# First MLP pair by plain products, and a down projection that begins without residuals

## Chip, cores and metric

One core of a Trainium2 chip. The metric is the device time of one execution in microseconds (us). Five engines run side by side, each with its own instruction stream: TensorE (PE, weight loads PEld), VectorE (DVE), ScalarE (ACT), GpSimd (POOL) and SyncE (SP, which here only issues DMAs).

## What is computed

One inference step of a hybrid backbone with one trunk layer: 1152 tokens (128 of context, 1024 latent), 1024 channels, all float32.

```python
def trunk_layer(x, mod, lp, lam, lam_init, ctx_k, ctx_v, rope):
    shift1, scale1, gate1, shift2, scale2, gate2 = jnp.split(mod, N_MOD, axis=-1)
    h = rmsnorm(x, lp['w_norm1']) * (1.0 + scale1) + shift1
    mix, k, v = token_mixer(h, lp, lam, lam_init, ctx_k, ctx_v, rope)
    x = x + gate1 * mix
    h = rmsnorm(x, lp['w_norm2']) * (1.0 + scale2) + shift2
    up = dwconv(h @ lp['w_up'], lp['w_ffn_dw'])
    ff = (jax.nn.silu(up[..., :D_FF]) * up[..., D_FF:]) @ lp['w_down']
    x = x + gate2 * ff
    return x, k, v
```

The token mixer (attention and a convolution, merged by gates, with an output projection at its end) is not touched. The change lies in the part from `gate1 * mix` on: the second norm, the MLP's up projection to 2 x 2816 channels, a depthwise convolution of width 3 over tokens, the gate, and the down projection.

## The kernel before

**Layout and precision.** Activations lie with channels on the 128 partitions and tokens along the free axis, in three thirds of 384 tokens (`n` = 0, 1, 2; third 0 holds the context tokens, so it has two segments with different modulation). Each float32 operand is split into a rounded part `hi` (ScalarE's cast) and a remainder `lo` (a subtraction on VectorE or POOL), and a product is three matmuls: hi·hi, hi·lo, lo·hi. Weights come in units of 128 x 1024: SP's queue loads `raw`, ScalarE casts `whi` (L180), POOL subtracts `wlo` (L182); `prep_to` does this some units ahead, with four buffers each for `whi` and `wlo`.

**Order.** The program is written in the order wanted, with a clock of *ticks*: `run` and `block` tick after a number of matmuls, and `defer(t, f)` emits the step `f` `t` ticks later. A background list `bg` is emitted at `bg_rate` per tick, and `flush` ticks until nothing is pending. At build time a scheduler with a timing model of its own fixes the order of each engine's instructions; it may move them against the written order (`pin` limits that to 144 instructions on PE and 24 on VectorE). On the chip each engine runs its own instructions in that order and waits at the first whose inputs aren't there.

**Output projection** (`out_and_ffn`, `wo_unit`). Eight units for thirds 0 and 1, then the same eight for third 2 (24 matmuls each, a tick per 8). VectorE adds the gated result to the residual `x1[n]` (`resid`, L1230), ScalarE squares it (L1243), VectorE adds up the squares (L1244). A copy of `x1` goes to DRAM (`xscr`) for the last residual add. During the first eight units VectorE also reduces modulation vectors from their weight matrix (`ada2`, L1192).

**Second norm.** For each third the sum of squares is summed over partitions by TensorE (`stat_cols`, L252: three products with one column each), VectorE adds epsilon, POOL takes the power, VectorE makes a diagonal (L265), TensorE broadcasts it into PSUM (`stat_bcast`, L273). Then VectorE multiplies (`mulr`, L1300) and ScalarE scales and shifts in place (`affine`, L1306). All steps for thirds 0 and 1 are deferred by 1, 2, 3, ... ticks into the output projection of third 2.

**Up projection in pairs** (`mlp`, `pair`). Pair `i` makes 128 channels of each half of `w_up` for all tokens. For thirds 0 and 1 it takes the 2 x 2 scheme of Strassen and Winograd: the two halves of the contraction, the two channel blocks and the two thirds form 2 x 2 blocks, and seven products of 12 matmuls (`block`) take the place of eight. For this `mlp_operands` makes seven operands from quarters of the normalised tokens: B11, B22, B21 as they are, nT1, T2, nT3, nT4 as sums and differences (VectorE and POOL), each then split into hi and lo (`split`, L1322, L1323). The sums of weight quarters are VectorE's too (`fetch_pair`, L164). Third 2 is computed plainly in four blocks `c1` to `c4`. Seven PSUM banks rotate; VectorE combines the products (`tt`, L1472), then come the depthwise filter `dw` (ScalarE L1432, VectorE L1434), silu (L1530) and the product of both halves (L1532), which goes to DRAM (`fscr`). After pair 0, `stage` starts the reduction of the last modulation vector, which gates the MLP's result, in the background (L1192, in bursts of four).

**Down projection** (`down`, then the last group with the final norm). The 22 channel blocks of `fscr` are taken in groups: first 2, then five times 4. Each is loaded (L1565), cast (L1566) and split (L1568) by `ff_prep`; group 0 multiplies 24 banks with 6 matmuls each, the later groups 24 with 12 each; `resid` adds each bank, gated, to `x1`. The residuals `x1` are loaded back from `xscr` during the last pair (`reload`, L1551), into the slots of operands that are used up by then. PSUM gives five banks here.

Of the kernel before, what the change touches and what calls it, by code (L numbers as in the profile page):

```python
# [8 lines left out]
F32 = mybir.dt.float32  # L9
# [7 lines left out]
NCTX = 128  # L17
# [4 lines left out]
KC = 8  # L22
# [61 lines left out]
def _w_order():  # L84
# [8 lines left out]
    ffn = [f"w{i}_{u}" for i in range(NFF) for u in range(4)] + down  # L93
# [16 lines left out]
class Kernel:  # L110
# [1069 lines left out]

    def ada2(self, count, more=True):
        nc = self.nc
        for _ in range(count):
            u, raw = self.ada_raw.pop(0)
            ty, k = divmod(u, KC)
            b = self.vec[:, V_ADA + 16 + u:V_ADA + 17 + u]
            step = self.junk.shape[-1]
            for c in range(2):
                acc = self.mod[:, ty, k, c:c + 1]
                for o in range(0, 1024, step):  # L1190
                    sl = slice(o, o + step)
                    nc.vector.tensor_tensor_reduce(out=self.junk, in0=raw[:, sl], in1=self.cbc[c][:, sl], scale=0.5,  # L1192
                                                   scalar=acc if o else b, op0=ALU.mult, op1=ALU.add, accum_out=acc)
            if more:
                self.defer(3, lambda: self.ada_fetch(1))


    def out_and_ffn(self):
        tc, nc, A = self.tc, self.nc, self.A
        vec = self.vec  # L1200
        with tc.tile_pool(name="p3", bufs=1) as p3:
# [35 lines left out]

            def square(n, j):
                if j == 0:
                    nc.scalar.activation(out=acc[n], in_=x1[n][:, 0], func=AF.Square)  # L1240
                else:
                    sq = self.sm.tile([128, CH], F32, tag="dg", name="sq", bufs=2)
                    nc.scalar.activation(out=sq, in_=x1[n][:, j], func=AF.Square)  # L1243
                    nc.vector.tensor_tensor(out=acc[n], in0=acc[n], in1=sq, op=ALU.add)  # L1244

# [31 lines left out]
            for i, f in enumerate(op["steps"]):  # L1277
                self.defer(1 + i, f)
            for j in range(KC):
                wo_unit(j, (2,))  # L1280
            self.flush()
            for i, f in enumerate(self.third_operands(x1, acc, op)):
                self.defer(1 + i, f)
            self.mlp(p3, x1, op, hx, slot, small, flat, resid)

    def norm_steps(self, acc, bank, col_bank, box):
# [8 lines left out]
        return [a, a2, b]  # L1295

# [12 lines left out]
    def mlp_operands(self, x1, acc, hx):  # L1309
# [16 lines left out]
        s0 = self.norm_steps(acc[0], lambda: self.spare[:, 0], lambda: self.spare[:, 2], box[0])  # L1326
        s1 = self.norm_steps(acc[1], lambda: self.spare[:, 1], lambda: self.spare[:, 2], box[1])
        steps = [s0[0], s1[0], s0[1], s1[1], s0[2], s1[2]]
        x, y = x1[0], x1[1]

        def half(q):
            up, dn = slice(2 * q, 2 * q + 2), slice(4 + 2 * q, 6 + 2 * q)

            def m(rows):
                def f():
                    for n in range(2):
                        self.mulr(x1[n], rows, box[n]["r"])
                    for n in range(2):
                        for k in range(rows.start, rows.stop):
                            self.affine(n, x1[n], k)  # L1340
                return f
# [461 lines left out]
```

## Time and profile before

| | us |
|---|---|
| median of 3 runs | 1833.96 |
| lowest and highest | 1832.01, 1837.11 |
| the profiled execution | 1833.82 |
| its span, first to last instruction | 1832.0 |
| TensorE busy in it | 1689.6 |

The profile is of one execution. A stretch is named by its start and end in us from the first instruction. "Idle before <- releaser" gives how long an engine had nothing to run before an instruction and what ended that; engine, line and tile of the releaser stand behind the arrow. TensorE's clock is the granted one, as a share of full speed; it has two levels, 0.5 and 1.

### The profile page before, as it was taken

The numbers are of one execution on the slowest core, as the hardware profiler recorded it, in microseconds if no ns is written. First come the engines' busy times: TensorE is split into PE (matmuls) and PEld (weight loads), VectorE is DVE, ScalarE is ACT, GpSimd is POOL, SyncE is SP. The second block draws the span as 40 slices with busy tenths as digits, with TensorE's granted clock in tenths as the row PEclk, the third lists the DMA queues.
The fourth block names the chain that finished last, engine by engine and source line by source line (L and its number), as shares of the span: only waits on it lengthen the run. The fifth ranks groups of instructions, "written<-read, shape, count | busy, mean of one in ns | idle before, by whom it ended". The sixth has DMA issues, their size and how long they took to land. (4 is left out here: it accounts for less than half of the span.)

```text
span 1832.0 us, 25186 instructions
## 1 busy us (share of the span) xinstructions
PE 1689.6 (92%) x9874; PEld 1646.4 (90%) x9874; DVE 1265.6 (69%) x1620; ACT 681.6 (37%) x1073; POOL 820.2 (45%) x479
## 2 busy tenths in 40 slices
PE   5989899989989999899985998999999996999997
PEld 3889889988989999789985998999999996999997
DVE  5858985697795762786879878786766856433335
ACT  4423444354553563211254433334333433111111
POOL 2545782674872422543345533444444543233211
PEclk8999999999999999999987999999999998999999
DMA  8264233433425325665831322221212226222202
GB/s 316 75 186 144 90 94 96 146 80 116 119 80 196 116 95 193 196 214 193 293 129 37 100 95 90 71 85 67 84 54 72 79 100 245 97 99 70 89 12 104
DMA packets 101295, 220.50 MB, mean 120 GB/s; under 512 B 9876, under 2 KB 60728, under 8 KB 98744
## 3 DMA queue, kind: packets, MB, share of 16 engines
q1 hardware_dynamic: 48720, 136.66, 21.8%
q10 hardware_dynamic: 51592, 79.08, 13.6%
q0 software_dynamic: 864, 3.15, 0.5%
q8 instruction: 78, 1.28, 0.3%
q14 instruction: 41, 0.34, 0.1%
HBM read 161.55 MB, written 57.30 MB: 119 GB/s over the span
## 5 line engine op out<-in xcount | busy, mean ns | idle before, releaser
L182 POOL TENSOR_TENSOR wlo<-raw,whi 128x1024 fp32r<-128x1024 f32 x124 | 328.0, 2646 | 532.7 <-ACT whi L180 515.3
L230 PE MATMUL f<-h1h,whi 128*128 128x384 f32 x680 | 233.2, 345 | 4.6 <-ACT gt L602 3.2
L230 PE MATMUL f<-h1l,whi 128*128 128x384 f32 x680 | 233.9, 344 | 0.0
L1434 DVE SCALAR_TENSOR_TENSOR X<-X,vec,X 128x1153 f32<-128x1153 f32 x88 | 164.6, 1871 | 98.4 <-ACT X L1432 97.6
L230 PE MATMUL f<-h1h,wlo 128*128 128x384 f32 x680 | 231.5, 341 | 0.0
L180 ACT CAST whi<-raw 128x1024 fp32r<-128x1024 f32 x126 | 131.8, 1046 | 231.8 <-PE f L230 50.0
L639 DVE SCALAR_TENSOR_TENSOR conv<-glu,vec,conv 128x967 f32<-128x967 f32 x120 | 199.2, 1660 | 1.1
L182 POOL TENSOR_TENSOR wlo<-rawx,whi 128x1024 fp32r<-128x1024 f32 x44 | 112.3, 2559 | 88.6 <-ACT whi L180 80.1
L652 POOL TENSOR_TENSOR conv<-conv,tap 128x200 f32<-128x200 f32 x120 | 115.5, 963 | 69.4 <-ACT tap L646 66.9
L230 PEld LDWEIGHTS f<-h1h,whi 128*128 128x128 f32 x680 | 130.0, 192 | 6.6 <-ACT gt L602 3.9
L230 PEld LDWEIGHTS f<-h1l,whi 128*128 128x128 f32 x680 | 130.4, 192 | 0.4
L230 PEld LDWEIGHTS f<-h1h,wlo 128*128 128x128 f32 x680 | 129.8, 191 | 0.2
L781 DVE TENSOR_REDUCE mx<-S 128x1 f32<-128x1152 f32 (+1 forms) x72 | 88.6, 1231 | 31.4 <-PE S L775 31.4
L783 ACT ACTIVATE e<-S,mx 128x1152 f32<-128x1152 f32 (+1 forms) x72 | 81.3, 1129 | 69.8 <-DVE mx L781 58.1
L230 PE MATMUL T<-ff,whi 128*128 128x384 f32 x360 | 94.1, 339 | 14.2 <-ACT ff L1566 11.6
L646 ACT ACTIVATE tap<-glu,vec 128x200 f32<-128x200 f32 x120 | 55.5, 462 | 106.0 <-POOL conv L652 89.2
L180 ACT CAST whi<-rawx 128x1024 fp32r<-128x1024 f32 x44 | 46.0, 1051 | 129.1 <-DVE rawx L164 60.2
L230 PE MATMUL f<-ff,whi 128*128 128x384 f32 x340 | 88.5, 338 | 0.0
L774 PE MATMUL S<-K,q 128*128 128x384 f32 (+1 forms) x200 | 69.1, 346 | 13.9 <-ACT e L783 13.9
L230 PEld LDWEIGHTS T<-ff,whi 128*128 128x128 f32 x360 | 66.1, 191 | 15.4 <-ACT ff L1566 12.0
L1230 DVE SCALAR_TENSOR_TENSOR hx<-T,g,hx 128x128 f32<-128x128 f32 (+1 forms) x79 | 38.9, 513 | 57.8 <-PE T L230 57.6
L1230 DVE SCALAR_TENSOR_TENSOR hx<-f,g,hx 128x384 f32<-128x384 f32 (+1 forms) x76 | 37.6, 514 | 57.6 <-PE f L230 57.6
(419 smaller groups left out, 4890.7 us busy)
## 6 DMA issues: line engine op xcount, KB each, us to landing
raw<-in_wst SPq DMA_DIRECT2D x104, 512.0 KB, 4.0
X<-scr_fscr SPq DMA_DIRECT2D x22, 576.0 KB, 4.7
scr_fscr<-X SPq DMA_DIRECT2D x22, 512.0 KB, 2.9
scr_gscr<-gate ACTq DMA_DIRECT2D x48, 192.0 KB, 2.0
tg<-scr_gscr SPq DMA_DIRECT2D x24, 384.0 KB, 4.3
ada<-in_ada SPq DMA_DIRECT2D x8, 1024.0 KB, 9.9
araw<-in_ada ACTq DMA_DIRECT2D x16, 512.0 KB, 4.1
K<-scr_kscr ACTq DMA_DIRECT2D x4, 1920.0 KB, 7.8
```

The lines of the kernel that those rows point to most:

```text
L180: nc.scalar.copy(hi, raw)
L182: eng.tensor_tensor(out=lo, in0=raw, in1=hi.bitcast(F32), op=ALU.subtract)
L230: nc.tensor.matmul(out, lhsT=a, rhs=b, start=(i == 0), stop=(i == n - 1))
L639: t = nc.vector.scalar_tensor_tensor(out=o, in0=glu[:, j:j + CSPLIT], scalar=w[:, j:j + 1], in1=o, op0=ALU.mult, op1=ALU.add)
L646: nc.scalar.activation(out=p, in_=glu[:, CSPLIT + j:CONVW + j], func=AF.Copy, scale=w[:, j:j + 1])
L652: t = nc.gpsimd.tensor_tensor(out=o, in0=o, in1=p, op=ALU.add)
L774: nc.tensor.matmul(S[:, j, :cw], lhsT=qt[:, c, o:o + 128], rhs=self.K[:, c, ks], start=True, stop=False)
L781: nc.vector.tensor_reduce(out=mx[:, 1:2], in_=src, axis=AX.XY, op=ALU.min)
L783: nc.scalar.activation(out=e[:, :w].rearrange("p (a b) -> p a b", a=nk), in_=src, func=AF.Exp, scale=-1.0, bias=mx[:, 1:2], accum_out=self ...
L1230: nc.vector.scalar_tensor_tensor(out=d, in0=ps[:, o:o + ln], scalar=gate[:, j, c:c + 1], in1=d, op0=ALU.mult, op1=ALU.add)
L1434: nc.vector.scalar_tensor_tensor(out=y[:, :L], in0=u[:, t:t + L], scalar=w[:, t:t + 1], in1=y[:, :L], op0=ALU.mult, op1=ALU.add)
```

## The change

- Pair 0 no longer uses the seven products. `first_pair` multiplies the unchanged weights `fa0` and `fb0` with the tokens as they are: twelve blocks, thirds 0, 1, then 2. Its operands are B11, B21, B12 and B22, made by `h2_rows` during the output projection of third 2; for third 0 ScalarE writes `hi` directly from the scale-and-shift, and VectorE makes the same value again for the remainder.
- The sums of quarters (`op["sums"]`) follow in the ticks of `first_pair`, after and between the steps for third 2; all their splits are now on VectorE. nT4 takes the buffer of B12 at the end.
- The norm's steps start at tick 4 instead of 1; the flush before `mlp` is gone; third 2's squares are summed by TensorE as each is made.
- The background reduction begins after pair 1 and goes piece by piece, one each 10 ticks.
- Loads of `fscr` are issued by `ff_load`: the first two from SP at the end of the pair before the last, the others from POOL, each as soon as its buffer's last user is written down.
- Group 0 of the down projection writes `x1` by ScalarE (`begin`), and POOL issues accumulating DMAs that add the residuals from `xscr`, two rows of a third at a time. `reload` is gone.

```diff
-    ffn = [f"w{i}_{u}" for i in range(NFF) for u in range(4)] + down
+    ffn = up[:2] + [f"w{i}_{u}" for i in range(1, NFF) for u in range(4)] + down
...
             def square(n, j):
-                if j == 0:
+                if n == 2:
+                    sq = self.sm.tile([128, CH], F32, tag="dg", name="sq", bufs=2)
+                    nc.scalar.activation(out=sq, in_=x1[n][:, j], func=AF.Square)
+                    self.defer(2, lambda: add_square(sq, j))
+                elif j == 0:
...
             for i, f in enumerate(op["steps"]):
-                self.defer(1 + i, f)
+                self.defer(4 + i, f)
             for j in range(KC):
                 wo_unit(j, (2,))
-            self.flush()
-            for i, f in enumerate(self.third_operands(x1, acc, op)):
-                self.defer(1 + i, f)
+            for i, f in enumerate(self.third_operands(x1, sums, op)):
+                self.defer(2 + i, f)
+            for i, f in enumerate(op["sums"]):
+                self.defer(6 + i, f)
             self.mlp(p3, x1, op, hx, slot, small, flat, resid)
...
+    def h2_rows(self, n, x, rows, r, hi, lo, direct):
+        nc = self.nc
+        self.mulr(x, rows, r)
+        if direct:
+            for k in range(rows.start, rows.stop):
+                for o, ln, c in self.segs(n):
+                    nc.scalar.activation(out=hi[:, k - rows.start, o:o + ln], in_=x[:, k, o:o + ln], func=AF.Identity,
+                                         scale=self.s2[:, k, c:c + 1], bias=self.h2s[:, k, c:c + 1])
+                    nc.vector.tensor_scalar(out=x[:, k, o:o + ln], in0=x[:, k, o:o + ln],
...
+        else:
+            for k in range(rows.start, rows.stop):
+                self.affine(n, x, k)
+            nc.scalar.copy(hi, x[:, rows])
+        nc.vector.tensor_tensor(out=lo, in0=x[:, rows], in1=hi.bitcast(F32), op=ALU.subtract)
...
+        steps += [plain(n, q, d) for d in range(2) for q in range(2) for n in range(2)]
...
+            def o2():
+                tt(x[:, up], x[:, up], y[:, up], ALU.subtract)
+                split("nT1", up, x[:, up], nc.vector)
+            def o4():
+                tt(x[:, up], x[:, up], y[:, dn], ALU.add)
+                split("T2", up, x[:, up], nc.vector)
+                tt(x[:, dn], x[:, dn], x[:, up], ALU.subtract)
+            def o5():
+                tt(y[:, up], y[:, up], y[:, dn], ALU.subtract)
+                split("nT3", up, y[:, up], nc.vector)
+            def o7():
+                if q == 0:
+                    op["nT4"] = op["B12"]
                 split("nT4", up, x[:, dn], nc.vector)
...
-            self.bg = [lambda: self.ada2(1)] * 8 + [lambda: nc.vector.tensor_copy(self.g2, self.mod[:, 3])]
-            self.bg_rate = (1, 20)
+            self.bg = [f for _ in range(8) for f in self.ada2_steps()]
+            self.bg += [lambda: nc.vector.tensor_copy(self.g2, self.mod[:, 3])]
+            self.bg_rate = (1, 10)
...
+        def first_pair():
...
+            for n in range(NCH):
+                for u in range(2):
+                    for k0 in (0, 4):
+                        quarter(u, n, k0)
+                if n == 1:
+                    self.prep_to(self.pos + 2)
+            up = flat(slot("X2"))
...
+            for u in range(2):
+                for n in range(NCH):
+                    to_u(up[u], n, lambda d, t: nc.scalar.copy(d, bank[u, n][:, t]))
+            self.flush()
+            for f in ops["late"]:
+                f()
+            start()
...
+            dw(0, up[0], ya)
+            nc.scalar.activation(out=ya[:, :1153], in_=ya[:, :1153], func=AF.Silu)
+            dw(NFF, up[1], yb)
...
-            if i == 0:
+            if i == 1:
                 stage()
+            if i == NFF - 2:
+                ff_load(), ff_load()
...
-        def reload(n):
-            x1[n] = hx()
-            nc.sync.dma_start(out=x1[n], in_=A["xscr"][n])
+        def ff_load():
+            c = parts_at["stage"]
+            parts_at["stage"] += 1
+            if c < NFF:
+                raw = late["x2"][:, T * (c % 2):T * (c % 2) + T]
+                (nc.sync if c < 2 else nc.gpsimd).dma_start(out=raw, in_=A["fscr"][c])
...
+        def begin(n, j, ps):
+            if j == 0:
+                x1[n] = hx()
+            for o, ln, c in self.segs(n):
+                nc.scalar.activation(out=x1[n][:, j, o:o + ln], in_=ps[:, o:o + ln], func=AF.Copy,
+                                     scale=self.g2[:, j, c:c + 1])
+            if j % 2:
+                sl = slice(j - 1, j + 1)
+                nc.gpsimd.dma_start(out=x1[n][:, sl], in_=A["xscr"][n][:, sl], accum_op=ALU.add)
...
-                    resid(n, j, ps, self.g2)
+                    if g:
+                        resid(n, j, ps, self.g2)
+                    else:
+                        begin(n, j, ps)
...
-        for i in range(NFF):
+        first_pair()
+        for i in range(1, NFF):
             pair(i)
```

## Rows read from the trace of the kernel before

**Rows 1.** the page's first part: busy us, share of the span, instructions

```profile
PE 1689.6 (92%) x9874; PEld 1646.4 (90%) x9874; DVE 1265.6 (69%) x1620; ACT 681.6 (37%) x1073; POOL 820.2 (45%) x479
```

**Rows 2.** stretches: length, busy us per engine (count), TensorE clock, DMA share, GB/s

```profile
920.00:967.00 47.00, 39.62 (x221) 39.29 (x219) 33.41 (x50) 28.24 (x48) 21.16 (x11) 0.89 0.36 123
967.00:1020.00 53.00, 34.31 (x155) 32.01 (x154) 42.59 (x43) 23.22 (x32) 34.13 (x22) 0.77 0.12 41
1020.00:1046.00 26.00, 22.93 (x121) 22.00 (x120) 25.79 (x29) 11.44 (x13) 10.44 (x4) 0.93 0.42 131
1046.00:1300.00 254.00, 243.62 (x1383) 240.47 (x1382) 200.02 (x245) 93.78 (x106) 109.97 (x42) 0.99 0.24 81
...
1520.00:1545.00 25.00, 10.75 (x44) 9.64 (x43) 14.37 (x17) 9.29 (x9) 9.72 (x4) 0.69 0.90 332
1545.00:1780.00 235.00, 235.00 (x1353) 235.00 (x1353) 92.97 (x178) 42.59 (x43) 70.08 (x30) 1.00 0.23 80
```

**Rows 3.** TensorE's timeline: start us, us, line, operation [idle us before <- releaser]

```profile
929.55 1.44 PE L252 MATMUL S<-cols,acc 128*128 128x1 f32 x6 [7.38 <-DVE acc L1244]
...
936.64 0.72 PE L252 MATMUL S<-cols,acc 128*128 128x1 f32 x6
937.23 0.42 PE L230 MATMUL O<-ml,whi 128*128 128x384 f32 x1
```

**Rows 4.** TensorE's waits in 960:1046, 1046:1300, 1515:1560: us, times, longest

```profile
PE f L1442 <- POOL wlo L182: 5.7, 1, 5.7
...
PE O L1442 <- DVE X L1472: 5.1, 2, 4.7
...
PE T L1442 <- POOL wlo L182: 1.8, 1, 1.8
...
PE T L230 <- ACT ff L1566: 11.6, 1, 11.6
PE T L230 <- DVE hx L1230: 2.4, 1, 2.4
```

**Rows 5.** timeline of SP's queue before the down projection

```profile
1517.21 1.26 SPq L1551 DMA_DIRECT2D hx<-scr_xscr  x2
...
1519.06 0.97 SPq L1565 DMA_DIRECT2D X<-scr_fscr  x2
```

**Rows 6.** timelines of VectorE and POOL: start us, us, operation, count

```profile
944.70 6.99 DVE L1300 TENSOR_TENSOR X<-X,S 128x768 f32<-128x768 f32 x8
...
964.13 5.13 DVE L1323 TENSOR_TENSOR hx<-X,hx 128x768 fp32r<-128x768 f32 x2
...
1111.11 2.72 DVE L1192 CUSTOM_DVE_ANT_0 X<-X,vec 128x512 f32<-128x512 f32 x1
...
948.55 2.41 POOL L182 TENSOR_TENSOR wlo<-raw,whi 128x1024 fp32r<-128x1024 f32 x1 [4.20 <-ACT whi L180]
...
964.08 6.83 POOL L1323 TENSOR_TENSOR op<-X,op 128x768 fp32r<-128x768 f32 x3 [1.11 <-ACT op L1322]
```

**Rows 7.** single lines of the kernel: duration ns min/median/max, starts, forms

```profile
L1323 DVE TENSOR_TENSOR hx<-X,hx x6: 939/1644/2619, 952.7 to 990.6; 128x768 fp32r<-128x768 f32 x6
...
L288 DVE TENSOR_SCALAR mn<-mn,s,h1s x32: 333/468/2631, 26.4 to 76.1; 128x384 f32<-128x384 f32 x16, 128x128 f32<-128x128 f32 x8, 128x256 f32<-128x256 f32 x8
...
L164 DVE TENSOR_TENSOR raw<-raw x22: 674/679/693, 960.1 to 1480.3; 128x512 f32<-128x512 f32 x22
...
L180 ACT CAST whi<-raw x126: 1027/1048/1067, 16.4 to 1763.4; 128x1024 fp32r<-128x1024 f32 x126
...
L182 POOL TENSOR_TENSOR wlo<-raw,whi x124: 2339/2406/4181, 52.2 to 1764.5; 128x1024 fp32r<-128x1024 f32 x124
...
L1434 DVE SCALAR_TENSOR_TENSOR X<-X,vec,X x88: 1407/1423/3543, 1019.3 to 1524.9; 128x1153 f32<-128x1153 f32 x88
...
L1505 ACT COPY X<-f x7: 472/473/484, 1017.4 to 1419.4; 128x384 f32<-128x384 f32 x7
```

**Rows 8.** the view of DMA issues: count, KB each, us to landing

```profile
X<-in_crow POOLq DMA_DIRECT2D x2, 512.0 KB, 6.7
```

More of the change, by code (lines that the diff above doesn't have):

```diff
@@ L1244, in square, with add_square @@
                     nc.vector.tensor_tensor(out=acc[n], in0=acc[n], in1=sq, op=ALU.add)
+            def add_square(sq, j):
+                if j == 0:
+                    sums["ps"] = self.spare[:, 2]
+                for t in range(3):
+                    nc.tensor.matmul(sums["ps"][:, t:t + 1], lhsT=sq[:, t * 128:(t + 1) * 128], rhs=self.col_mean,
+                                     start=j == 0 and t == 0, stop=j == KC - 1 and t == 2)
             cb, ar = flat(hx()), flat(hx())
@@ L1325, in mlp_operands, with part @@
         box = [{}, {}]
[L1326 to L1327 removed]
+        s0, s1 = (self.norm_steps(acc[n], b, b, box[n]) for n, b in
+                  enumerate((lambda: self.spare[:, 0], lambda: self.spare[:, 1])))
         steps = [s0[0], s1[0], s0[1], s1[1], s0[2], s1[2]]
         x, y = x1[0], x1[1]
+        def part(name, q):
+            rows = slice(2 * q, 2 * q + 2)
+            return op[name][:, rows], op[name][:, rows.start + 4:rows.stop + 4]
@@ new lines, in alloc, with plain, f @@
+        def alloc():
+            for name, make in (("B11", hx), ("nT1", hx), ("T2", hx), ("B22", hbt), ("nT3", hbt), ("B21", hbt),
+                               ("B12", hbt)):
+                operand(name, make)
+        def plain(n, q, down):
+            def f():
+                if not op:
+                    alloc()
+                hi, lo = part(f"B{2 if down else 1}{n + 1}", q)
+                rows = slice(4 * down + 2 * q, 4 * down + 2 * q + 2)
+                self.h2_rows(n, x1[n], rows, box[n]["r"], hi, lo, n == 0)
+            return f
@@ L1343, in o1 @@
-            def o1():
-                if q == 0:
-                    for name, make in (("B11", hx), ("nT1", hx), ("T2", hx), ("B22", hbt), ("nT3", hbt),
-                                       ("B21", hbt), ("nT4", hbt)):
-                        operand(name, make)
-                split("B11", up, x[:, up], nc.vector)
-            def o2():
-                nc.vector.tensor_tensor(out=x[:, up], in0=x[:, up], in1=y[:, up], op=ALU.subtract)
-                split("nT1", up, x[:, up], nc.vector)
@@ L1379, in third_operands @@
+        h0, h1 = half(0), half(1)
+        return {"steps": steps, "ops": op, "sums": [f for ab in zip(h0[0], h1[0]) for f in ab], "late": [h0[1], h1[1]]}
+    def third_operands(self, x1, sums, ops):
         nc = self.nc
+        op = ops["ops"]
         hi = op["h"] = self.hb.tile([128, KC, CH], F32R, tag="hb", name="h2h")
@@ L1403, in mlp, with edges @@
         late = {}
+        def edges(tiles):
+            for t in tiles:
+                for c0 in (0, 129, 1154):
+                    nc.gpsimd.memset(t[:, c0:c0 + 1], 0.0)
+            return tiles
         def start():
```

132 lines of the change are left out of this document (64 added, 68 removed).

## The prediction

> **What bounds the kernel now.** The page's first part comes first: TensorE is busy for 92% of the span [rows 1], so the time is TensorE's, and a change can win only its waits and its slow stretches. The view of stretches shows where they lie [rows 2]: from 1545 us to 1780 us TensorE is busy all the time at clock 1.00; between 920 and 1046 us, and again between 1520 and 1545 us, it is not. The steady price is 235.00 us / 1353 = 0.1737 us for a matmul of 384 columns. For each stretch the idle time is its length less TensorE's busy time, and the slowness, which the lower granted clock leaves, is busy time less count x 0.1737 us; TensorE's waits name what ended the longest idle pieces [rows 4]. All by [rows 2]:
>
> - 920 to 967 us (output projection of the third tokens): idle 47 - 39.6 = 7.4, nearly all before the column sums of squares [rows 3]; slow 39.62 - 221 x 0.1737 = 1.2.
> - 967 to 1046 us (first two MLP pairs): idle 79 - 34.31 - 22.93 = 21.8, the longest for a weight split of POOL (5.7 [rows 4]); slow 57.24 - 276 x 0.1737 = 9.3.
> - 1046 to 1300 us: idle 10.4; slow 243.62 - 1383 x 0.1737 = 3.4.
> - 1520 to 1545 us (start of the down projection): idle 14.2, of it 11.6 for ScalarE's cast of the MLP's result and 2.4 for VectorE's eviction [rows 4]; slow 10.75 - 44 x 0.1737 = 3.1.
>
> That is 70.8 us in all, and the change touches each of the four. Stages before 920 us stay as they are.
>
> **Part 1, the statistics.** TensorE's first wait, 7.4 us, is for the last sum of squares of token third 0 [rows 3]. This step moves from the first tick to the fourth. A tick is 8 matmuls here, so 24 x 0.1737 = 4.2 us of work goes ahead of it, and 3.2 us of waiting stay: gain 4.2. The squares of the third tokens are now summed by TensorE as they come: ten sets of three one-column products in place of three. A set holds the matmuls up by 0.59 us (936.64 to 937.23 us [rows 3]), so 7 x 0.59 = 4.1 us are added. The additions that VectorE loses by it gain nothing by themselves.
>
> **Part 2, plain products in the first pair.** Seven products of 12 matmuls and four blocks of 12 for the third tokens, 132, become twelve blocks, 144: 12 x 0.1737 = 2.1 us added for certain. In return the first blocks need only normalised tokens, no sums of quarters. For these VectorE has, while the third tokens' projection runs (192 matmuls, 33 us), per quarter two multiplications by the broadcast and two subtractions at 0.94 and four scale-and-shift pieces at about 0.4 (the same operation took 0.33 to 0.47 in the first norm) [rows 7]: 4 x 5.4 = 21 us, begun when the broadcasts are out, which I put 8 us behind the column sums of 929.55 us [rows 3], near 938. With the projection's evictions beside it, that ends at about 965 us: the operands are there when TensorE comes. ScalarE's part is covered: it idles 19 of the 47 us [rows 2].
>
> Then TensorE has eight blocks, 16.7 us, on token thirds 0 and 1. In them VectorE makes the third tokens' operands (8 operations) and the quarter sums and their splits (14), 22 x 0.94 = 21 us in alternation, begun some 5 us in. The third operands are done after 16 to 20 us: 0 to 3 us late. The weight sums of pair 1 stand behind the quarter sums, at 26 us; sum (0.68), cast (1.05) and POOL's split (2.41) [rows 7] make 30 us, where TensorE wants them at 25: 5 us late. In pair 1 the depthwise filters of pair 0 (four of 1.42 [rows 7]) stand before the later weight sums: 0 to 6, say 2. With 3 us at the lower clock behind these waits, 12 of the 31.1 us stay: gain 19. Bounds: 3 stay if all operands are early (gain 28), 24 if VectorE lags (gain 7).
>
> VectorE and POOL hinder each other: two of its subtractions took 5.13 us at 964.13 us while POOL ran three of its own [rows 6], against 0.94 each at best [rows 7]; its multiplications by a PSUM operand kept 0.87 each through POOL's work at 948.55 us [rows 6]. The change takes 6 splits of 2.4 us off POOL here and gives them to VectorE. The Trainium skill (SBUF — State Buffer, "Who interferes with whom") states that a VectorE instruction with two SBUF inputs and a GpSimd instruction that reads SBUF exclude each other for the whole instruction, and that one with a single SBUF input does not; the trace agrees with both (5.13 and 0.87 us). The rival that follows from it is the first below.
>
> **Part 3, modulation spread out.** After pair 0 the last modulation vector is reduced in the background, four pieces in a burst each 20 ticks; now one piece each 10 ticks, from the end of pair 1. At 1111.11 us such a piece took 2.72 us ahead of a weight sum [rows 6], and TensorE waited 1.8 us for the weight; its longest wait here, 4.7 us for VectorE's eviction, lies among such pieces too [rows 4]. Only these two carry the mark of the bursts: 6.5 us and part of the slow 3.4. New backlog from pair 1 eats some: gain 5, bounds 0 and 10.
>
> **Part 4, start of the down projection.** The load behind TensorE's wait of 11.6 us was issued at 1519.06 us, after two reloads of residuals on SP's queue [rows 5], in a stretch with the DMA engines 90% busy [rows 2]. The change takes the reloads away and issues the first two loads a pair (23 us) earlier, so the casts fit into the last pair. That cover needs POOL, whose split of the odd part (2.4 us or more [rows 7]) must find room among the weight splits of the last pair; a weight split takes 2.41 and four fall in its 23 us. Late next is ScalarE: it now drains the first group's 24 banks, 8 x (2 + 1 + 1) copies at 0.47, 15 us, with eight casts of 1.05, 8.4 [rows 7], and the last pair's silu and filter ahead of them: 24 us or more beside TensorE's 144 x 0.1737 = 25 us. And a cast that waits for its load holds the copies queued behind it, as VectorE's queue was held before (2.4 us [rows 4]). I leave 4 of the 17.3 us: gain 13, bounds 1 and 10 left.
>
> The later loads go from SP's queue to POOL's: no gain, since TensorE doesn't wait in the later groups (235 of 235 us busy [rows 2]); POOL's splits now stand behind a load that waits for its buffer, covered by POOL's 165 idle of 235 us.
>
> The twelve accumulating DMAs that POOL issues replace the reloads. The trace has none. Nearest are POOL's own loads of 512 KB, 6.7 us from issue to landing [rows 8], so 5 us for 384 KB as a plain load, and up to double if the target is read and written. A first-group value is wanted by the second group's eviction 23 us after it is written, the last ones 40 us after. I take 0, by that row; bounds 0 and the second rival.
>
> **Sum.** -4.2 + 4.1 + 2.1 - 19 - 5 - 13 = -35. The profiled execution took 1833.82 us (its span 1832.0), 0.1 below the median of the runs, so 1833.8 - 35 = **1799 us**.
>
> **Rivals.**
> - *VectorE and POOL stay the bound.* From 922 us to the end of pair 1 (87 us of matmuls) POOL has some 17 weight splits of 2.41, 41 us. VectorE has 28 operand operations of 0.94, 12 weight sums of 0.68 and the filters (7), all with two SBUF inputs: 41 us. If these exclude each other, 82 of the 87 us are gone, and VectorE's other 30 us must all lie over POOL's. If half of them do, it is 97 us, 10 later than TensorE: then 24 of part 2 stay, 1811 us. For: the 5.13 us [rows 6]. Against: POOL sheds 14 us of operand splits. Chance 0.19.
> - *The accumulations are late: slower.* Landing one after another at L us, the twelfth ends 5 + 12 L after the first group starts, and the eviction wants it at 66: VectorE waits, the banks fill, TensorE stops. It begins to cost from L = 5.1 and outweighs the 35 us from L = 8. At 10 us it is 125 - 66 = 59 us of waiting, 1858 us. For: a single queue. Against: POOL's two 512 KB loads were issued together and both landed in about 7 us [rows 8], so they overlap. Chance 0.05. By the Trainium skill (DMA: Bandwidth & Descriptors, "Anatomy of one DMA — SWDGE (gpsimd) path") a DMA of this kind takes 2.0 us plus bytes / 436 GB/s, an estimate of 2.9 us, which would be no wait; its "Rules for kernel authors" adds that an accumulate also reads its destination.
> - *The down start stays held up*, by ScalarE's or POOL's order: 10 of the 17.3 stay, 1805 us. For: ScalarE's 24 us or more of 25. Chance 0.13.
> - *All operands are early*: gains 4.2 + 28 + 8 + 15 less the 6.2 added, 1785 us. Against: the weight sums' place. Chance 0.12.
> - *It doesn't do what it says*: the build's scheduler puts the operand steps behind the first pair's turn, the old waits stay with 6 us added, and only part 4 gains: 1827 us. Chance 0.04.
>
> **How the numbers follow.** The forecast has 0.47; with the bounds of part 3 and a few us in part 2 and 4 it spans 1790 to 1808 by itself. The range goes to 1783 and 1815: it takes in all but the late accumulations and the change without effect, and loses some tails. About 0.3% (5.5 us) is what a measurement of this kernel can tell from no change. Faster by more: all cases but the accumulations and half of the last, 0.93. Within it 0.03, slower 0.04.
>
> **What would show it.** Right: TensorE's wait before the first column sums is about 3 us; the first MLP matmuls run on thirds 0 and 1 with no wait for VectorE or POOL; waits in the first two pairs sum to about 8 us; the down projection starts within 2 us of the last pair; no eviction of the second down group waits for a DMA. Wrong: waits of 10 us or more for POOL's weight splits in pair 1, ScalarE's copies held by a cast that waits for a load, or evictions held by an accumulation.

## The result, and the profile after

The changed kernel takes 1811.7 us (median of four runs, 1807.9 to 1816.1) where the kernel before takes 1834.6 beside it: ratio 0.9876, interval 0.9849 to 0.9903. It is faster by some 22 us; 35 were forecast, and the time lies within the range, near its upper end. The profiled execution took 1811.61 us, span 1809.8, so 22.2 less than that of before.

The page's first part [rows 1] after the change, and the same stretches as [rows 2] (length, busy us of PE, PEld, DVE, ACT and POOL with counts, granted clock, DMA share, GB/s):

```profile
PE 1690.3 (93%) x9928; PEld 1649.2 (91%) x9928; DVE 1253.8 (69%) x1594; ACT 691.0 (38%) x1106; POOL 819.0 (45%) x507
...
920.00:967.00 47.00, 42.87 (x248) 42.55 (x247) 35.63 (x56) 23.39 (x38) 22.03 (x11) 0.93 0.43 146
967.00:1020.00 53.00, 46.58 (x261) 45.42 (x260) 44.51 (x55) 32.62 (x49) 15.98 (x20) 0.94 0.11 36
1020.00:1046.00 26.00, 24.46 (x140) 23.93 (x139) 22.83 (x23) 10.81 (x12) 11.88 (x5) 1.00 0.36 118
1046.00:1300.00 254.00, 243.31 (x1372) 241.77 (x1371) 196.23 (x240) 91.81 (x104) 107.91 (x41) 0.98 0.24 80
1300.00:1520.00 220.00, 213.63 (x1219) 212.35 (x1218) 155.77 (x175) 87.16 (x102) 104.59 (x43) 0.99 0.26 87
1520.00:1545.00 25.00, 22.96 (x131) 22.32 (x130) 14.44 (x9) 19.50 (x35) 21.57 (x20) 1.00 1.02 257
```

One stretch of before was not among the rows, and it turns out to matter:

```profile
1300.00:1520.00 220.00, 219.12 (x1264) 218.80 (x1263) 150.32 (x167) 83.21 (x94) 99.26 (x38) 1.00 0.24 79
```

The counts tell how far TensorE has come at a given time. Up to 1046 us it has issued 649 instructions instead of 497. Of the 152 more, 42 are the one-column products of part 1 (seven sets, six instructions each in the trace), and 12 are matmuls that only the plain pair has. So it is (152 - 42 - 12) x 0.1737 = 17.0 us ahead, which is to the tenth what the forecast's parts 1 and 2 give (-4.2 + 4.1 + 2.1 - 19). Between 1046 and 1300 us it issues 1372 instead of 1383 and falls back by 1.9; between 1300 and 1520 us 1219 instead of 1264, back by another 7.8. At the start of the down projection, 131 instead of 44, it gains 15.1. Sum: 17.0 - 1.9 - 7.8 + 15.1 = 22.4 us, and the spans differ by 22.2. **Two stages came out as forecast, one came out on the other side:** in the pairs between 1046 and 1520 us a gain of 5 was expected and 9.7 were lost. By the prediction's own measures, 5.8 of these are idle time (17.1 us instead of 11.3) and 3.9 slowness at the lower clock (6.9 instead of 3.0).

TensorE's waits after, in 915 to 1046 us, 1046 to 1500 us and 1500 to 1560 us (us in total, times, longest), against [rows 4]:

```profile
PE T L1487 <- ACT h2h L1335: 4.9, 1, 4.9
PE S L252 <- DVE acc L1259: 4.1, 1, 4.1
PE S L1487 <- DVE X L1563: 1.5, 1, 1.5
...
PE S L1487 <- DVE acc L1563: 6.6, 3, 2.9
PE S L1487 <- DVE X L1563: 5.5, 2, 3.0
PE f L1487 <- DVE X L1563: 3.2, 1, 3.2
...
PE T L230 <- ACT hx L1679: 1.5, 1, 1.5
```

The wait for the statistics is 4.1 instead of 7.4 us [rows 3]; POOL's 5.7 and ScalarE's 11.6 are gone. One wait of the first pair is new, 4.9 us for the third tokens' high halves. The middle group is what was not foreseen: 15 us for VectorE's evictions, mostly on the spare bank S, spread over the pairs up to 1480 us. Not all of it is new. Before, the pairs had 9.4 us of such waits, the 5.1 us of [rows 4] and these:

```profile
PE S L1442 <- DVE X L1472: 3.0, 5, 0.9
...
PE S L1442 <- DVE acc L1472: 1.3, 1, 1.3
```

The accumulating DMAs, and the plain loads that POOL issued among them, by issue view of 1519 to 1546 us (count, KB each, median us to landing):

```profile
hx<-scr_xscr POOLq DMA_DIRECT2D x12, 384.0 KB, 9.2
X<-scr_fscr POOLq DMA_DIRECT2D x4, 576.0 KB, 9.3
```

No eviction waited for one.

### The profile page after: what moved, and what is told of

The parts are those of the page before. It is cut to its first block, busy times and chain, and to the rows that moved or that the text cites. A ratio compares the mean times of both kernels' runs of the same rounds, so it can differ in the third digit from the quotient of the medians.

```text
span 1809.8 us, 25328 instructions
## 1 busy us (share of the span) xinstructions
PE 1690.3 (93%) x9928; PEld 1649.2 (91%) x9928; DVE 1253.8 (69%) x1594; ACT 691.0 (38%) x1106; POOL 819.0 (45%) x507
## 4 chain that ended last, share of the span: by engine, by line
PE 45%; DVE 22%; issue 9%; DMA 5%; ACT 4%; POOL 4%; ACTq 0%; POOLq 0%; SPq 0%; DVEq 0%
PE f L230 14%; PE T L230 7%; DVE conv L639 5%; PE S L1487 5%; PE T L1487 4%; PE f L1487 4%; PE O L230 3%; PE O L1487 2%; DVE X L1479 2%; DVE mx L781 2%; DMA tg<-scr_gscr 2%; PE O L822 2%; DVE S L1194 2%; DVE e L794 2%; POOL wlo L182 1%
## 5 line engine op out<-in xcount | busy, mean ns | idle before, releaser
L1479 DVE SCALAR_TENSOR_TENSOR X<-X,vec,X 128x1153 f32<-128x1153 f32 x88 | 159.1, 1812 | 75.8 <-ACT X L1477 75.2
L182 POOL TENSOR_TENSOR wlo<-rawx,whi 128x1024 fp32r<-128x1024 f32 x42 | 107.2, 2558 | 104.7 <-ACT whi L180 97.4
L811 DVE TENSOR_TENSOR atl<-T,ath 128x512 fp32r<-128x512 f32 (+1 forms) x100 | 52.0, 538 | 31.5 <-ACT ath L810 31.2
L1239 DVE SCALAR_TENSOR_TENSOR hx<-f,g,hx 128x128 f32<-128x128 f32 (+1 forms) x64 | 31.6, 515 | 58.8 <-PE f L230 58.7
L1239 DVE SCALAR_TENSOR_TENSOR hx<-T,g,hx 128x256 f32<-128x256 f32 (+1 forms) x66 | 32.4, 512 | 54.3 <-PE T L230 54.0
```

The costliest lines, as they stand in the source:

```text
L182: eng.tensor_tensor(out=lo, in0=raw, in1=hi.bitcast(F32), op=ALU.subtract)
L1239: nc.vector.scalar_tensor_tensor(out=d, in0=ps[:, o:o + ln], scalar=gate[:, j, c:c + 1], in1=d, op0=ALU.mult, op1=ALU.add)
L1479: nc.vector.scalar_tensor_tensor(out=y[:, :L], in0=u[:, t:t + L], scalar=w[:, t:t + 1], in1=y[:, :L], op0=ALU.mult, op1=ALU.add)
```

## The experiments

Each run is set beside runs of the kernel before on the same chip; ratios are to that kernel.

### Is the background sum the cause?

Two runs change part 3 alone. In one the background goes back to bursts of four pieces every 20 ticks (still from pair 1 on):

```diff
-            self.bg = [f for _ in range(8) for f in self.ada2_steps()]
-            self.bg += [lambda: nc.vector.tensor_copy(self.g2, self.mod[:, 3])]
-            self.bg_rate = (1, 10)
+            self.bg = [lambda: self.ada2(1)] * 8 + [lambda: nc.vector.tensor_copy(self.g2, self.mod[:, 3])]
+            self.bg_rate = (1, 20)
```

> The change with one part put back: the background reduction goes in bursts of four pieces each 20 ticks again (still from the end of pair 1). Theory A, the pieces themselves make TensorE's waits in the pairs, and spreading them over twice the time only doubled the time in which they collide with VectorE's evictions: the waits after about 1230 us go, 5 to 8 us in all, so about 1805 us. Theory B, the waits come from the changed phase of VectorE against POOL's weight splits, whatever the pieces do: same within 3 us, 1809 to 1815 us, with waits still at about 1314, 1388 and 1480 us. Theory of the prediction, that spreading gains 5 us: about 1817 us.

Measured: 1822.5 us, ratio 0.9921 [0.9906, 0.9935], slower than the change. Spreading gains 8 to 10 us by the ratios; theory A has the wrong sign here.

In the other the background sum is left out, and with it the last modulation vector (the gate is a copy of another one):

```diff
-            self.bg = [f for _ in range(8) for f in self.ada2_steps()]
-            self.bg += [lambda: nc.vector.tensor_copy(self.g2, self.mod[:, 3])]
+            self.bg = [lambda: nc.vector.tensor_copy(self.g2, self.mod[:, 2])]
```

> The change without the background reduction: the last modulation vector is not computed, the down projection is gated by a copy of another one. This prices all pieces together. Theory A (the pieces make the waits): most of the 24 us of TensorE's idle and slow time between 1046 and 1520 us goes, 15 to 20 us, so 1792 to 1797 us. Theory B (phase against the weight splits): 2 to 6 us, 1806 to 1810 us, and waits for VectorE's evictions of 2 to 3 us remain at several places.

Measured: 1802.1 us, 0.9814 [0.9799, 0.9828]. All pieces together cost 9 to 10 us, between the theories. But the waits on S were all still there and hardly shorter, 6.0 us in three for `acc` and 4.7 in two for `X`. So the pieces are not what makes those waits.

### Are the sums of quarters the cause?

```diff
-                self.defer(6 + i, f)
+                self.defer(11 + i, f)
```

> The change with the quarter sums deferred by five more ticks. In the changed kernel TensorE waited 6.4 us for the third tokens' operands, whose first VectorE step came 5 us after its column sums were done, behind quarter sums. Theory C, the sums' place on VectorE makes that wait: it falls below 2 us and with the lower clock behind it 6 us are gained, about 1806 us. Rival: the sums are then late for pair 1 (nT1, T2) or the weight sums slide, and the wait only moves to pair 1: 1809 to 1814 us.

Measured: 1808.3 us, 0.9849 [0.9832, 0.9865]: at most a few us, not resolved. The wait for the high halves stayed at 4.5 us. But the sums did not come later on VectorE either: the build's scheduler put them forward again, the first to 952 us (963 in the changed kernel), and all eight ran before the high halves. So this run does not test theory C.

### What is part 4 worth?

The reloads on SP, VectorE's additions in the first group and the late loads are put back:

```diff
+                nc.sync.dma_start(out=raw, in_=A["fscr"][c])
                 nc.scalar.copy(fh, raw)
...
-                    if g:
-                        resid(n, j, ps, self.g2)
-                    else:
-                        begin(n, j, ps)
+                    resid(n, j, ps, self.g2)
```

> The change with part 4 undone: residuals reloaded on SP's queue during the last pair, loads of the MLP's result on SP's queue when their cast is due, VectorE evicting the first down group. Prediction's theory: part 4 alone is worth 13 to 15 us, so 1825 to 1827 us, with TensorE waiting about 11 us for ScalarE's first cast. Rival: the down start is late by another cause that the rest of the change mended as well: less than 8 us, below 1820 us.

Measured: 1819.7 us, 0.9910 [0.9895, 0.9925]. By the ratios part 4 seems worth 6 to 8 us only, though its stretch had gained 15.1. With it undone TensorE waits 7.2 us there, where the kernel before waited 14.2, so the rest of the change had already taken away about half of that wait; by what is not shown.

### A new theory: the weight slots

None of the four touched the late evictions, so the pairs themselves were compared. VectorE and POOL of the changed kernel, ahead of the eviction that TensorE waits for at 1315 us (start, us, operation):

```profile
1302.44 2.61 DVE L1479 SCALAR_TENSOR_TENSOR X<-X,vec,X 128x1153 f32<-128x1153 f32 x1 [2.11 <-ACT X L1477]
1304.97 2.89 DVE L164 TENSOR_TENSOR raw<-raw 128x512 f32<-128x512 f32 x1
1307.78 4.90 DVE L1479 SCALAR_TENSOR_TENSOR X<-X,vec,X 128x1153 f32<-128x1153 f32 x2
...
1316.49 0.55 DVE L1563 TENSOR_TENSOR acc<-S,acc 128x384 f32<-128x384 f32 x1
...
1299.05 2.42 POOL L182 TENSOR_TENSOR wlo<-rawx,whi 128x1024 fp32r<-128x1024 f32 x1 [3.03 <-ACT whi L180]
1301.42 2.41 POOL L182 TENSOR_TENSOR wlo<-raw,whi 128x1024 fp32r<-128x1024 f32 x1
1303.80 3.52 POOL L182 TENSOR_TENSOR wlo<-rawx,whi 128x1024 fp32r<-128x1024 f32 x1
1309.07 2.40 POOL L182 TENSOR_TENSOR wlo<-raw,whi 128x1024 fp32r<-128x1024 f32 x1 [1.76 <-ACT whi L180]
```

The first of the next pair's weight sums takes 2.89 us instead of 0.68, and a depthwise tap 2.45 instead of 1.42 [rows 7], because POOL's low halves run just then. And the order of those is odd: a pair's units are loaded into `raw`, `rawx`, `rawx`, `raw`, and here a `raw` (the fourth unit) goes ahead of the second `rawx` (the third). In the order of POOL's instructions this happens in three pairs of the changed kernel, seven pairs apart, and in the kernel before in none behind the first two pairs. The scheduler had exchanged them. The code has a place where it could have got another input: hi and lo tiles come from a cycle of four slots, three of the common pool and one private (`cycle((self.wp, self.wp, self.wp, p3))`). The plain first pair takes two units where the old one took four, which turns every later unit by two slots against the cycle. One line turns it back for the pairs. It is set before the output projection, though, so it also turns the slots of that stage's weights, which the change had left as they were:

```diff
-            self.wring = cycle((self.wp, self.wp, self.wp, p3))
+            self.wring = cycle((self.wp, p3, self.wp, self.wp))
```

The changed kernel itself was run again beside it,

> The changed kernel itself, unedited, beside the kernel before on this chip, so that the next runs have their base in the same call. Every theory expects 0.9876 of the kernel before again (0.985 to 0.990), about 1812 us.

(1811.0 us, 0.9866 [0.9852, 0.9881]), then the changed kernel with that line,

> The changed kernel with the four weight slots of the last stage taken in another order (second slot first from the private pool instead of the fourth), so that each unit of a pair again uses the slot that it used before the change; no arithmetic differs. Theory D (the first pair now takes two units instead of four, which turned the slots against the units; in every seventh pair POOL then makes the low halves of a pair's third and fourth unit in the other order, they run beside VectorE's taps and weight sums and stretch them, and the eviction that the spare bank waits for is late): the waits at about 1137 and 1143 us (1.0 and 2.9), 1315 (1.8) and 1480 (1.9) go, POOL's low halves go back to the order of before in all pairs; 7 us less than the changed kernel, 1803 to 1807 us. The waits at about 1219 (3.0) and 1388 (2.4), whose pairs have the old order already, stay under D. Rival E (the pairs wait because VectorE is late from the first pair on, whatever the slots): the waits stay, within 3 us of the changed kernel. Rival F (the waits follow from which accumulator bank a product falls on, shifted by the first pair's six banks): no change, within 3 us.

and the kernel before with that line alone:

> The mirror of the last one: the kernel before, with its weight slots of the last stage taken in the changed order and nothing else. Theory D: some pairs between 1046 and 1520 us get the order that the changed kernel had in three of its pairs, and with it waits on a spare bank of 2 to 4 us each: 4 to 10 us slower than before, 1839 to 1845 us. Rivals E and F: no change, within 3 us.

Measured: the changed kernel with its slots turned back takes **1792.8 us**, 0.9768 [0.9753, 0.9782], 18 us less. The kernel before with its slots turned takes 1843.0 us, 1.0041 [1.0026, 1.0056], 6.7 us more. Both lie on theory D's side, the second within its figure; the first is more than twice the 7 us expected. Rivals E and F, which expected no change, fall. Stretches of the first (length, busy us of PE, clock, DMA share, GB/s):

```profile
920.00:967.00 47.00, 46.59 (x290) 1.00 0.37 128
967.00:1020.00 53.00, 46.75 (x256) 0.94 0.21 66
1020.00:1046.00 26.00, 22.33 (x126) 1.00 0.20 75
1046.00:1300.00 254.00, 249.11 (x1419) 0.99 0.25 82
1300.00:1520.00 220.00, 215.75 (x1239) 1.00 0.32 103
1520.00:1545.00 25.00, 25.00 (x146) 1.00 1.04 278
```

Against the changed kernel that is 23 instructions more up to 1046 us, 47 up to 1300, 20 up to 1520 and 15 up to 1545: 4.0 + 8.2 + 3.5 + 2.6 = 18.3 us, all of the gain. Of it 11.7 lie between 1046 and 1520 us. The pairs gained 2.3 more, since this kernel's waits at the start of the down projection (1.5 and 0.8 us) already lie before 1520 us and those of the changed kernel behind it: 14.0 us. The 4.0 us up to 1046 us are no restoration: nearly all is the wait for the first column sums (below), in the output projection, where the line makes an order that neither the kernel before nor the changed one had.

The mirror run shows both effects apart (against [rows 2]):

```profile
920.00:967.00 47.00, 41.11 (x225) 0.93 0.31 109
967.00:1020.00 53.00, 38.59 (x185) 0.77 0.18 62
1020.00:1046.00 26.00, 23.11 (x124) 0.93 0.31 105
1046.00:1300.00 254.00, 236.62 (x1311) 0.97 0.23 78
1300.00:1520.00 220.00, 215.32 (x1232) 0.99 0.22 76
```

Up to 1046 us it gains 37 instructions, 6.4 us, with the same line; in the pairs it loses 72 + 32, 18.1 us, far more than the total of 6.7 shows. The order of POOL's instructions goes with the slots: it differs in three of the later pairs in each of the six profiles of the changed kernel with the turned slots and in the mirror run, and in none of the six with the slots turned back.

The pair of above, 15 us earlier now:

```profile
1288.65 6.47 DVE L1479 SCALAR_TENSOR_TENSOR X<-X,vec,X 128x1153 f32<-128x1153 f32 x3
1295.04 0.68 DVE L164 TENSOR_TENSOR raw<-raw 128x512 f32<-128x512 f32 x1
...
1296.97 2.90 DVE L1194 CUSTOM_DVE_ANT_0 X<-X,vec 128x512 f32<-128x512 f32 x1
...
1301.69 0.55 DVE L1563 TENSOR_TENSOR acc<-S,acc 128x384 f32<-128x384 f32 x1
...
1286.68 2.41 POOL L182 TENSOR_TENSOR wlo<-rawx,whi 128x1024 fp32r<-128x1024 f32 x1 [6.73 <-ACT whi L180]
1289.30 3.28 POOL L182 TENSOR_TENSOR wlo<-raw,whi 128x1024 fp32r<-128x1024 f32 x1 [0.20 <-ACT whi L180]
```

Third unit, then fourth, and POOL is done when the weight sum comes: 0.68 us. TensorE's wait is 0.52 us where it was 1.82. The collision has not gone altogether: now a background piece takes 2.90 us where it took 0.74, and from the first tap shown to the end of the eviction it is 13.6 us instead of 14.6. Over all pairs this sum (the first of a pair, `raw` from `raw`) has a median of 0.68 us in both kernels. Its three long cases with the turned slots, 2.85 to 2.89 us, lie in the three exchanged pairs; the longest with the others is 0.69. The mirror run has three as well, 1.9 to 2.9 us:

```profile
L164 DVE TENSOR_TENSOR raw<-raw x19: 673/678/2886, 1051.5 to 1491.7; 128x512 f32<-128x512 f32 x19
```

The other sums of a pair take up to 2.9 us in each of these kernels. Of the waits that theory D named (1.0 and 2.9 us near 1140, 1.8 at 1315, 1.9 at 1480) 0.5 of 7.6 us are left.

The waits at 1219 and 1388 us of the changed kernel (3.0 and 2.4), which theory D left in place, fell to 1.9 and 0.9 too, and the waits of the first column sums from 4.1 to 0.4. So the slots do more than this exchange. For the column sums, which come ahead of the pairs, one difference shows: VectorE's small copy of a modulation vector took 2.36 us beside a POOL split, 0.16 with the other slots, where POOL was idle. That this is all of the 4.0 us is not shown, nor what in the scheduler turns a slot into another order.

### The third operands again, with the sums last

On the changed kernel with its slots turned back, the sums are meant to be set aside until the first pair's products are all issued:

```diff
-                self.defer(6 + i, f)
+                self.defer(26 + i, f)
```

> As the run with the old slots, and the sums of token quarters set aside until the first pair's products are all issued (26 ticks instead of 6), so that the mean of the third tokens' squares no longer stands behind five of them on VectorE. Theory C (the third operands came late because of these sums): the wait for the third high halves (4.9 us in the changed kernel) falls under 1.5, and the lower clock behind it goes; the eight sums run later, so pair 1 may wait for an operand up to 5 us: between the same and 6 us less than the run with the old slots alone, 1798 to 1806 us. If the third chain is bound by ScalarE and POOL instead (the inverse root took 4.1 us there), the wait stays at 4 to 5 us and the time is that of the run with the old slots or up to 4 us more.

Measured: 1790.9 us, 0.9762 [0.9745, 0.9779], not to be told from the run without it. TensorE's wait for the high halves grew from 4.9 to 6.7 us. That is no evidence against theory C, because the scheduler put the sums forward again: all eight run before the high halves, six of them behind the column sums (four without this edit). The chain of the third operands here (VectorE, POOL, VectorE, ScalarE), with some of the sums (L1396):

```profile
971.21 0.14 DVE L255 TENSOR_SCALAR ms<-S 128x3 f32<-128x3 f32 x1
971.28 3.95 DVE L1396 TENSOR_TENSOR X<-X,X 128x768 f32<-128x768 f32 x2
...
973.51 1.56 POOL L257 TENSOR_TENSOR rs<-ms,cols 128x3 f32<-128x3 f32 x1
...
976.63 0.67 DVE L265 TENSOR_SCALAR dg<-cst,rs 128x128 f32<-128x128 f32 x3
...
977.21 2.68 DVE L1396 TENSOR_TENSOR X<-X 128x768 f32<-128x768 f32 x3
...
981.56 3.54 DVE L1341 TENSOR_TENSOR X<-X,S 128x768 f32<-128x768 f32 x4
...
984.94 0.81 ACT L1335 CAST h2h<-X 128x768 fp32r<-128x768 f32 x1
```

The last column sums end at 967.6 us and the first high halves at 985.8: 18.2 us, of which little is the chain's own work. Each small step queues behind splits, weight sums and quarter sums on VectorE, or a weight split on POOL. Theory C, that the sums make this wait, fits these lines but stays untested.

### Each part once more, with the slots out of the way

Part 4 undone (the edit shown above):

> The changed kernel with the weight slots in the old order (0.9768 of before), and part 4 undone: the token quarters of the attention sum are loaded again in the last pair, the first group of the down projection adds them on VectorE, and the activations are loaded by SP when they are split. The prediction's term for part 4 (13 us of waits at the start of the down projection): 0.984 of before, about 1806 us. As undone beside the late pairs (0.9910 against 0.9866, 8 us): 0.981, about 1801 us. If part 4 moves only waits that the start has anyway: within 3 us of the run with the old slots, 1790 to 1796 us.

Measured: 1804.0 us, 0.9816 [0.9789, 0.9842]: part 4 is worth 9 us by the ratios, 11 by the medians. This run's waits at the start of the down projection:

```profile
PE T L230 <- ACT ff L1652: 5.9, 1, 5.9
PE T L230 <- DVE hx L1239: 2.9, 1, 2.9
```

They are 5.9 and 2.9 us, where the kernel before had 11.6 and 2.4 [rows 4].

Bursts again:

> The changed kernel with the weight slots in the old order, and part 3 undone alone: the background sums run in bursts of four pieces every 20 ticks, from pair 1 on. The prediction's term for spreading (5 us, bounds 0 and 10): 0.9795 of before, 1796 to 1800 us, with bursts seen as waits of 2 to 5 us between 1046 and 1230 us. If the 8 to 10 us that bursts cost beside the turned slots were the two together: within 3 us of the run with the old slots. If pieces are what makes VectorE late: under 1790 us.

Measured: 1813.8 us, 0.9868 [0.9837, 0.9899]: 18 us slower by the ratios, far over the 5 us of the prediction and outside its bounds. It all lies where the bursts run:

```profile
1046.00:1300.00 254.00, 235.73 (x1305) 0.97 0.22 73
```

114 instructions fewer than with single pieces, 19.8 us, in waits of 1 to 3 us for evictions by VectorE and by ScalarE.

The third tokens' squares on VectorE again:

```diff
-                if n == 2:
+                if n == 3:
...
-            for i, f in enumerate(self.third_operands(x1, sums, op)):
+            for i, f in enumerate(self.third_operands(x1, acc, op)):
...
-        return [a] + self.norm_steps(None, self.st, None, box)[1:] + [c(q) for q in range(4)]
+        return self.norm_steps(sums[2], self.st, self.st, box) + [c(q) for q in range(4)]
```

> The changed kernel with the weight slots in the old order, and the third tokens' squares added on VectorE again (one set of three column products instead of eight, so seven sets less on TensorE, eight additions less spared on VectorE). By the prediction's terms TensorE has 7 x 0.59 = 4.1 us less to do, and if VectorE has room for 7 more additions of about 0.5 us the time falls to 1788 or 1789 us; if VectorE is what the last quarter of the output projection and the first pair wait for, these additions (4 us, and the chain of the third operands begins behind them) come back whole: 1793 to 1800 us, with a longer wait for the third high halves than 4.9 us.

Measured: 1800.6 us, 0.9793 [0.9768, 0.9818]: 5 us slower by the ratios, 8 by the medians, although TensorE has seven sets less. The two intervals overlap (0.9753 to 0.9782 without this edit), so the size is uncertain. The new wait is an eviction of the output projection:

```profile
PE O L1487 <- DVE X L1239: 5.8, 1, 5.8
```

The wait for the high halves did not grow (4.3 us), but they come 8 us later, and the column sums of the third tokens end at 988 us instead of 972: the edit moves the statistics as well as the additions.

And no background at all (the same part of the computation left out as before):

> The changed kernel with the weight slots in the old order and the background sums left out (the gate is a copy of another vector). What single pieces still cost where the slots are in the old order: if as much as beside the turned slots (0.9866 against 0.9814, 9 to 11 us), 0.972 of before, 1782 to 1785 us, and the waits that remained at 1044 (3.2), 1163 (1.2) and 1208 us (1.9) go; if the spread hides nearly all of them (3 us or less), 0.975 to 0.978, 1789 to 1794 us, and those waits stay.

Measured: 1786.5 us, 0.9726 [0.9702, 0.9751], 6 to 8 us under the run with pieces, between the two figures. The wait at 1163 us went; those at 1044 and 1208 us (3.2 and 1.9) are 1.9 and 2.4 here.

Of the kernels that compute the whole, the fastest are the change with its slots turned back, 1792.8 us, and that with the sums set aside as well, 1790.9: 2.3 to 2.4% under the kernel before.

## Why the prediction was right, and where it was not

**Right in result, and in the two stages it spent most on.** In part that is luck. The sum gave 1799 us and by itself spanned 1790 to 1808; 1811.7 lies in the part of the range that was there for the rivals.

- *Part 1.* The wait came to 4.1 us against 3.2 forecast, and a set of column products holds TensorE up by 0.6 us as reckoned. But "the additions that VectorE loses by it gain nothing by themselves" does not hold up: with them back, and the statistics later by it, the time is 5 to 8 us worse, with a wait of 5.8 us for an eviction. By these figures TensorE's 4.1 us bought some 9 to 12 of VectorE's lateness.
- *Part 2.* Idle and slow together fell as forecast, to the tenth in the account of instructions. The 5.7 us for POOL are gone and the first eight blocks run without a wait. That it is to the tenth is luck, for the terms inside were off: the third operands came 4.9 us late and not 0 to 3, and no wait for a weight showed in pair 1, where 5 us were reckoned.
- *Part 4.* The start of the down projection gained 15.1 us in its stretch, against 13. Undone alone it is worth 6 to 8 by the ratios with the turned slots and 9 to 11 with the others, so part of the 15.1 belongs to the rest of the change. ScalarE's copies took 0.50 to 0.56 us each at the median (all widths) and not 0.47; TensorE waited 1.5 and 0.6 us for them, 4 were allowed.
- *The accumulations* cost nothing, as taken, but not for the price assumed. They landed in 9.2 us at the median, 5.8 at least, and not in about 5 (nor in the 2.9 of the second rival's estimate); one after another at the median price would have meant the slow rival. They overlapped, as POOL's two plain loads had suggested [rows 8]: issued between 1521.0 and 1545.8 us, the slowest 16.6 us to landing, all twelve were in after 41 us at most, where twelve times 5.8 would be 70.

**Wrong: part 3, and everything else in the pairs between 1046 and 1520 us.** The step that failed is "gain 5, bounds 0 and 10". Measured was a loss of 9.7 us in this stretch, 14.7 short of the forecast; the 2.1 us by which the start of the down projection beat its 13 bring that to the 12.6 us by which the forecast time was too short. What stands behind it:

- The stretch was taken as changed by the background alone. The change also takes two weight units out of the sequence, which turns the cycle of weight slots by two for all later pairs. Turning it back recovers 18 us in all, 14.0 in the pairs; the same turn costs the pairs of the kernel before 18.1 us (6.7 in all). This edit was part of the diff and had no term in the sum. None of the prediction's rivals has it either: the first one forecast the right time, 1811 us, by VectorE and POOL holding each other up before 1046 us, where part 2 in truth gained all it should; that its figure came out is luck. Its mechanism was at work, in another place: a weight sum of 2.89 us beside a POOL split.
- The 5 us for spreading the background were too little for the changed kernel: bursts there cost 8 to 10 us by the ratios, and 18 with the slots turned back. But the forecast was against the bursts of the kernel before, which begin a pair earlier, and what those cost was not measured by itself; up to 1300 us the run with bursts did 78 instructions fewer than that kernel (1305 against 1383). So the 18 are not one to add to the sum above. With slots turned back and pieces spread, the pairs gain 4.2 us on the kernel before (11 instructions, 1.9 us, and the 2.3 us of waits that belong to the down projection), near the 5 that were forecast.

The Trainium skill's rule (SBUF — State Buffer, "Who interferes with whom"), that a VectorE instruction with two SBUF inputs and a GpSimd one that reads SBUF exclude each other, fits the 2.89 us against 0.68. The same section adds that copies in a two-port mode can be excluded too; the 128x16 copy of 2.36 us against 0.16 agrees if it ran in that mode, which no run shows.

**Open:** how the scheduler arrives at the exchanged order; what the rest of the slots' effect is (the waits at 1219 and 1388 us, most of the 4.0 us before 1046 us); why bursts cost more in the changed kernel than in the one before; whether the sums of quarters make the third operands late. By the kernel's rotation of banks, the product that waits at 1315 us uses the last spare bank and waits for the eviction of the one before it, as if they were one; that was not tried.

## What to carry to other kernels

Ask of every edit which cycles it advances (buffers, slots, banks) and not only which work it adds: a stage with identical code can lose 14 us because its units come to lie two slots further. When a stage that a change should not touch gets slower, compare the order of instructions on its engines before blaming the load. And a small loss for the bounding engine is worth paying where it relieves the one it waits for: 4.1 us of column products seem to have bought 9 us or more. Before a step is said not to matter, the trace must show that the edit moved it: the sums of quarters were put off twice, and the scheduler put them forward both times.

## What the hardware showed that was not expected

The accumulating DMAs of 384 KB into SBUF landed in 9.2 us at the median, about twice what was estimated from a plain load, and an issue kept POOL busy for 1.2 us. But that is not shown to be the price of accumulating: the four plain loads of 576 KB that POOL issued among them took 9.3 us and 1.2 us per issue at the median too, while behind 1550 us such loads took 4.8 and 0.57. What both had in common is the stretch, with the DMA engines busy throughout (share 1.02). Small operations are not safe from the POOL and VectorE exclusion, and it goes both ways: VectorE's 128x16 copy took 2.36 us instead of 0.16, and POOL's inverse root of 128x3 values took 4.10 us among VectorE's subtractions:

```profile
983.08 2.68 DVE L1396 TENSOR_TENSOR X<-X 128x768 f32<-128x768 f32 x3
985.69 0.95 DVE L1364 TENSOR_TENSOR hx<-X,hx 128x768 fp32r<-128x768 f32 x1
...
983.24 4.10 POOL L257 TENSOR_TENSOR rs<-ms,cols 128x3 f32<-128x3 f32 x1 [17.97 <-DVE ms L255]
```
